# Where two FFN passes meet: another bank is copied first, and the weight splits queue elsewhere

## The chip, the cores and the metric

The kernel runs on one core of one Trainium2 chip, as one program. The metric is the device time in microseconds (us) of one execution, and the time of a version is the median of its runs. Every duration below comes from one profiled execution of the kernel before.

## What is computed

The reference is a two-layer causal decoder trunk on an input of 512 tokens by 1024 features. Each layer has an attention mixer and then a gated FFN with a short causal convolution, and each part is normalised and added back to the input. The change is in the down projection of the FFN, in both layers:

```python
def conv_ffn(h, w_up, conv_w, conv_b, w_down):
    u = causal_dwconv(h @ w_up, conv_w, conv_b)
    gate, up = jnp.split(u, 2, axis=-1)
    return (jax.nn.silu(gate) * up) @ w_down      # (512, 2816) @ (2816, 1024)
```

## The kernel before, in words

**Exact products from pairs.** Every fp32 operand is split into a high part and a remainder. ACT casts the high part (line 83 for weights, line 225 for activations) and DVE subtracts it (lines 84 and 226). A product is then three matmuls on PE: high by high (line 320), remainder by high (321), high by remainder (322), in `mm3`. Names with h at the end (`wh`, `gh`) are high parts, names with l (`wl`, `gl`) are remainders.

**Down projection with seven products in place of eight.** The 2816 rows are 22 blocks, which are taken as 11 pairs, and the tokens are taken in two halves s = 0 and s = 1. In *phase one* the loop over k (11 steps) accumulates four PSUM banks for each half: d, a, b and c, eight products of three matmuls in a step, 24 matmuls. In the last step (k = 10) the four banks of a half are summed into the tile `uu`: ACT copies one bank (line 689) and DVE adds the other three (line 691). In *phase two* the loop over n (11 steps) goes on accumulating into a, b and c without clearing them, six products in a step in the order a, b, c of half 0 and a, b, c of half 1, 18 matmuls. So the first product of phase two into a bank must wait until that bank has been read for `uu`. I call this place the seam. Bank d is not written in phase two. At the end the outputs are bank a and `uu` less b or c.

**Where the weights come from.** `down_weights` makes one unit of weights at a time. In phase two the unit c of step n is loaded (line 347, queue of SP, into one of three buffers `wraw`), split, and subtracted from a kept tile by DVE (line 340); the result is unit d of step n, which is split too. The activations of phase two are split by `split_later` (lines 225 and 226), whose sources lie in the tiles `hold`. Some of these share their memory with the gain tiles, so the loads of the next gains (line 221) wait until those splits are done. `W.next` hands out a unit, and before that makes units up to `W.depth` ahead. The units that are ahead come earlier in the program's text, and the scheduler, which puts the instructions of each engine in an order, goes by the text, by what is ready in its own reckoning and by free buffers. In phase one the depth is 4; in the last step it is set to 2, so that no further unit is made there, and afterwards it is set back.

Each engine runs its instructions in the order that it was given. In the names of the built program, banks acc_5183 to acc_5186 are d, a, b and c of half 0 in layer 0, and acc_5187 to acc_5190 are the same of half 1. The line numbers below 690 are the same before and after.

Of the kernel before, what the change touches and what calls it, by code (L numbers as in the profile page):

```python
# [13 lines left out]
ALU = mybir.AluOpType  # L14
# [83 lines left out]
def trunk(tc, A, out):  # L98
    nc = tc.nc
    PE, ACT, DVE, POOL = nc.tensor, nc.scalar, nc.vector, nc.gpsimd  # L100

    with ExitStack() as top:
# [15 lines left out]
        def bank(tag, name, *shape):  # L118

            t = pp.tile([P, S], F32, tag=tag, name=name, bufs=BANKS[tag])  # L120
            if not shape:
                return t[:]
            n = math.prod(shape)
            names = "abc"[:len(shape)]
            return t[:, :n].rearrange(f"p ({' '.join(names)}) -> p {' '.join(names)}",
                                      **dict(zip(names, shape)))
# [90 lines left out]
        W = Weights(nc, wpool, units, 5)  # L217

        def gain(name, row):
            g = glob.tile([P, D], F32, tag="gain", name="gain", bufs=2)  # L220
            nc.sync.dma_start(g[:], A[name][row:row + 1, :].partition_broadcast(P))
            return g
# [51 lines left out]
        def part_of(t, ms, n, a, g, between=None, dve_first=False):  # L274

            c = slice(n * S, n * S + S)
            o = t[:, c]
            if isinstance(a, tuple):
                DVE.tensor_tensor(o, *a, ALU.subtract)
                a = o  # L280
            def product():
                DVE.tensor_tensor(o, a, g[:, c], ALU.mult)

            if dve_first:
                product()
            junk = chp.tile([P, D], BF16, tag="junk", name="junk", bufs=1)
            ACT.activation(junk[:, :S], a, AF.Square, scale=D ** -0.5, accum_out=ms[:, n:n + 1])  # L287
            if between:
                between()
            if not dve_first:  # L290
                product()

        def begin(pool=None, tag="s"):
            return ((pool or chp).tile([P, D], F32, tag=tag, name="t", **({"bufs": 2} if tag in ("z", "sp") else {})),
                    begin_sum())
# [91 lines left out]
        def ffn(layer, xnT, pending, final):  # L387
            with ExitStack() as es:
# [141 lines left out]
                def product(o, x, fresh):  # L530
                    nonlocal slot, w
                    if slot % 2 == 0:
                        w = W.next()
                    for k in range(4):
                        b = slice(slot % 2 * S + k * P, slot % 2 * S + (k + 1) * P)
                        xs = [v[:, k] if isinstance(x, list) else v[:, k * 256:(k + 1) * 256] for v in x]
                        mm3(o, w[0][:, b], w[1][:, b], *xs, fresh and k == 0, k == 3, not fresh)
                    slot += 1
# [119 lines left out]
                bk = {(m, s): bank(tags[m][s], "acc") for s in range(2) for m in "dabc"}  # L658
# [8 lines left out]
                def split_later():  # L667
                    k = LATER[len(later)]
                    g = g_tile()
                    if k in whole:  # L670
                        split(g[0][:, :768], g[1][:, :768], home(whole[k])[:, :768])
                    else:
                        vs = [x[:].rearrange("p (a b) -> p a b", b=P) for x in g]
                        for at, src in zip((slice(1, 4, 2), slice(0, 4, 2), slice(4, 6)), hold[k]):
                            split(vs[0][:, at], vs[1][:, at], src)
                    later.append(g)

                for k in range(HF):
                    if k == HF - 1:
                        depth, W.depth = W.depth, 2  # L680
                        uu = sp.tile([P, 2, S], F32, tag="y", name="uu")
                    w1, w2 = W.next(), W.next()
                    for s in range(2):
                        g = early[k]
                        for m, at, w, half in (("d", 7 - s, w2, 0), ("a", 3 - 2 * s, w1, 0),
                                               ("b", 2 - 2 * s, w2, 1), ("c", 5 - s, w1, 1)):
                            product(m, s, g, at, w, half, k == 0, k == HF - 1)
                        if k == HF - 1:
                            ACT.copy(uu[:, s], bk["d", s])
                            for m in "abc":  # L690
                                DVE.tensor_tensor(uu[:, s], uu[:, s], bk[m, s], ALU.add)  # L691
                    if k < 3:

                        ACT.copy(t2[k], w2[0][:, :S].bitcast(F32))
                        DVE.tensor_tensor(t2[k], t2[k], w2[1][:, :S].bitcast(F32), ALU.add)
                    if k >= HF - 3:
                        split_later()
                W.depth = depth
                PLAN = {"a": (lambda s: 3 - 2 * s, 0, 0), "b": (lambda s: 5 - s, 0, 1), "c": (lambda s: 2 - 2 * s, 1, 0)}

                def later_product(m, s, n, ws, part=slice(0, S), fresh=False):
                    at, w, half = PLAN[m]
                    product(m, s, later[n], at(s), ws[w], half, fresh and n == HF - TAIL, n == HF - 1, not fresh, part)

                early_q = []
                for n in range(HF - TAIL):
                    ws = [W.next(), W.next()]
                    if len(later) < HF:
                        split_later()
                    for s in range(2):  # L710
                        for m in "abc":
                            later_product(m, s, n, ws)
                    if n == 2:
                        g_post = gain("ffn_post_g", layer)
                        if not final:
                            g_next = gain("od_pre_g", 0)
                    if n == 4:
                        for z in range(2):
                            early_q.append(begin(sp, "y"))
                            part_of(*early_q[z], 1, uu[:, z], g_post)  # L720
                    if n == 5:
                        for i in ORDER:
                            X[i] = glob.tile([P, D], F32, tag=f"X{i}", name=f"X{i}")
                            nc.sync.dma_start(X[i][:], spill[i * P:(i + 1) * P, :])
# [3 lines left out]
                ws = [[W.next(), W.next()] for _ in range(TAIL)]  # L728
                nx = None if final else new_xnT()

                def bank_done(m, s, *part, between=None):
                    for n in range(TAIL):
                        later_product(m, s, HF - TAIL + n, ws[n], *part)
                        if between and n == 1:
                            between()
                    return bk[m, s]

                if final:
# [15 lines left out]
                    with tc.manual_schedule(engines={DVE.engine, ACT.engine, POOL.engine}):  # L754
# [3 lines left out]
                        a = bank_done("a", 0)  # L758
# [19 lines left out]
                        a = bank_done("a", 1)  # L778
# [1105 lines left out]

        xnT = even()
        xnT = ffn(0, *xnT, False)
        xnT = odd(*xnT)
        ffn(1, *xnT, True)


# [100 lines left out]
```

## Time and profile before

| | |
|---|---|
| median of 3 runs | 1109.82 us (1108.27 to 1109.95) |
| profiled execution | 1108.7 us |
| its span, first to last instruction | 1106.8 us, so 1.9 us lie around it |
| mean granted clock of PE | 0.998 |
| PE, DVE, ACT busy in the span | 99%, 81%, 58% |
| phase one of layer 0 ends, phase two begins | 516.9 us from the span's start |
| the same in layer 1 | 1054.5 us |

A row of the timeline gives start, duration, engine, source line, operation, tiles and shapes, and in brackets how long the engine stood idle before it and what ended that. Equal neighbours are merged with a count. PE is matmuls and PEld the loading of their stationary operand. The duration of a matmul is modelled and matmuls overlap, so the distance from start to start is what one costs. At both seams every matmul has its row, so matmuls can be counted there.

### The profile page before, as it was taken

Reading aid. Unit: us, or ns where it says so; the run is one execution under the profiler, and the core shown is the slowest. Engines: PE = TensorE matmul, PEld = TensorE weight load, DVE = VectorE, ACT = ScalarE, POOL = GpSimd, SP = SyncE. Lnnn points to the kernel's source line nnn. Section 1 sums busy time; section 2 is a strip of 40 time slices with the busy share of each in tenths; the row PEclk is TensorE's granted clock in tenths of the full one; section 3 lists DMA queues with packets and bytes.
Section 4 is the critical chain, followed back from the end, with each engine's and each line's share of the span. In section 5 each row is a group of like instructions: output and inputs, shape, how many; then the busy total and the mean of one; then the engine's idle time right before and its main releaser. Section 6 shows DMA issues by size and latency. Waiting matters only on the chain.

```text
span 1106.8 us, 17950 instructions
## 1 busy us (share of the span) xinstructions
PE 1097.0 (99%) x6688; PEld 953.7 (86%) x6688; DVE 897.5 (81%) x1509; ACT 642.0 (58%) x1094; POOL 129.5 (12%) x246
## 2 busy tenths in 40 slices
PE   9999999999999999999999999999999999999997
PEld 8876777898999999887888877888999999988876
DVE  6676676498999999999874765458989999999896
ACT  6555666346666665556544655555566666656562
POOL 3211043220000000000032111014100000000002
PEclk9999999999999999999999999999999999999999
DMA  7897898457556555354727999858756555534462
GB/s 273 262 240 210 230 291 229 112 182 190 186 177 191 178 183 181 124 181 138 247 84 262 287 295 302 212 175 243 197 157 191 182 179 184 188 122 157 152 209 77
DMA packets 72600, 217.51 MB, mean 197 GB/s; under 512 B 10048, under 2 KB 11200, under 8 KB 64320
## 3 DMA queue, kind: packets, MB, share of 16 engines
q1 hardware_dynamic: 61872, 147.99, 40.3%
q0 software_dynamic: 9920, 67.12, 24.2%
q10 hardware_dynamic: 720, 1.25, 0.3%
q8 instruction: 53, 0.87, 0.3%
q14 instruction: 35, 0.29, 0.1%
HBM read 208.95 MB, written 73.43 MB: 255 GB/s over the span
## 4 chain that ended last, share of the span: by engine, by line
PE 86%; DVE 8%; DMA 3%; ACT 2%; issue 1%; POOL 0%; POOLq 0%; DVEq 0%; SPq 0%; ACTq 0%
PE u L322 12%; PE u L320 12%; PE u L321 12%; PE acc L320 3%; PE acc L321 3%; PE acc L322 3%; DVE wl L84 3%; PE apt L320 3%; PE apt L321 3%; PE apt L322 3%; PE ao L320 2%; DMA wraw<-in_ffn_w_down 2%; PE ao L322 2%; PE ao L321 2%; PE aqk L320 1%
## 5 line engine op out<-in xcount | busy, mean ns | idle before, releaser
L84 DVE TENSOR_TENSOR wl<-wraw,wh 128x1024 fp32r<-128x1024 f32 x246 | 298.2, 1219 | 33.5 <-ACT wh L83 32.9
L83 ACT CAST wh<-wraw 128x1024 fp32r<-128x1024 f32 x246 | 254.1, 1046 | 105.4 <-PE u L321 23.9
L322 PE MATMUL u<-xh,wl 128*128 128x256 f32 (+1 forms) x640 | 194.9, 305 | 0.0
L321 PE MATMUL u<-xl,wh 128*128 128x256 f32 (+1 forms) x640 | 194.8, 305 | 0.0
L320 PE MATMUL u<-xh,wh 128*128 128x256 f32 (+1 forms) x640 | 194.5, 305 | 0.0
L322 PEld LDWEIGHTS u<-xh,wl 128*128 128x128 f32 x640 | 122.2, 191 | 5.5 <-DVE wl L84 0.7
L321 PEld LDWEIGHTS u<-xl,wh 128*128 128x128 f32 x640 | 122.2, 191 | 4.9
L320 PEld LDWEIGHTS u<-xh,wh 128*128 128x128 f32 x640 | 122.0, 191 | 5.0
L320 PE MATMUL u<-gh,wh 128*128 128x256 f32 x384 | 108.7, 283 | 0.0
L322 PE MATMUL u<-gh,wl 128*128 128x256 f32 x384 | 108.7, 283 | 0.0
L321 PE MATMUL u<-gl,wh 128*128 128x256 f32 x384 | 108.6, 283 | 0.0
L320 PE MATMUL acc<-wh,gh 128*128 128x512 f32 (+1 forms) x234 | 90.4, 389 | 0.6 <-DVE uu L691 0.6
L321 PE MATMUL acc<-wl,gh 128*128 128x512 f32 (+1 forms) x234 | 90.9, 388 | 0.0
L322 PE MATMUL acc<-wh,gl 128*128 128x512 f32 (+1 forms) x234 | 90.6, 387 | 0.0
L233 POOL TENSOR_TENSOR rv<-ms,epst 128x1 f32<-128x1 f32 x31 | 11.8, 382 | 619.0 <-ACT junk L287 287.6
L484 ACT ACTIVATE y<-u,cw 128x512 f32<-128x512 f32 x88 | 67.7, 777 | 26.5 <-PE u L322 26.4
L321 PEld LDWEIGHTS u<-gl,wh 128*128 128x128 f32 x384 | 73.7, 192 | 0.1
L320 PEld LDWEIGHTS u<-gh,wh 128*128 128x128 f32 x384 | 73.7, 192 | 0.1
L322 PEld LDWEIGHTS u<-gh,wl 128*128 128x128 f32 x384 | 73.7, 192 | 0.0
L163 POOL DMA_DIRECT2D ws<-in_ffn_up_q x72 | 51.8, 721 | 158.5 <-DMA ws<-ws 74.7
L490 DVE SCALAR_TENSOR_TENSOR y<-u,cw,y 128x510 f32<-128x510 f32 x88 | 65.5, 747 | 2.2
L488 DVE SCALAR_TENSOR_TENSOR y<-u,cw,y 128x511 f32<-128x511 f32 x88 | 65.1, 743 | 1.2 <-ACT y L484 1.2
(382 smaller groups left out, 2456.4 us busy)
## 6 DMA issues: line engine op xcount, KB each, us to landing
ws<-in_ffn_up_q POOLq DMA_DIRECT2D x48, 768.0 KB, 12.7
wraw<-ws SPq DMA_DIRECT2D x128, 256.0 KB, 2.9
wraw<-in_ffn_up_q SPq DMA_DIRECT2D x96, 256.0 KB, 2.9
wraw<-in_ffn_w_down SPq DMA_DIRECT2D x44, 512.0 KB, 3.5
ws<-ws POOLq DMA_DIRECT2D x16, 768.0 KB, 13.3
ws<-in_ffn_up_q POOLq DMA_DIRECT2D x24, 512.0 KB, 6.7
wraw<-in_ffn_w_up SPq DMA_DIRECT2D x24, 512.0 KB, 4.7
wraw<-in_od_w_dqk SPq DMA_DIRECT2D x12, 512.0 KB, 10.0
```

Of the source, the lines that this page charges most:

```text
L83: self.nc.scalar.copy(h[:, :w], raw[:, :w])
L84: self.nc.vector.tensor_tensor(l[:, :w], raw[:, :w], h[:, :w].bitcast(F32), ALU.subtract)
L163: nc.gpsimd.dma_start(tiles[j][c][:].rearrange(wide, q=4), src.rearrange(wide, q=4), accum_op=op, max_dma_last_dim=8192)
L233: POOL.tensor_tensor(v[:, :n], ms, eps[:, :n], ALU.add)
L320: PE.matmul(o, lh, rh, start=first, stop=False, skip_group_check=more)
L321: PE.matmul(o, lh, rl, start=False, stop=False, skip_group_check=more)
L322: PE.matmul(o, ll, rh, start=False, stop=last, skip_group_check=more)
L484: ACT.activation(y[:, z], u[z], AF.Identity, bias=c[:, 3:4], scale=c[:, 2:3])
L488: DVE.scalar_tensor_tensor(y[:, z, 1:], u[z][:, :S - 1], c[:, 1:2], y[:, z, 1:], ALU.mult, ALU.add)
L490: DVE.scalar_tensor_tensor(y[:, z, 2:], u[z][:, :S - 2], c[:, 0:1], y[:, z, 2:], ALU.mult, ALU.add)
```

## The change

Three things change in the text of `ffn`, and with it in both layers.

1. In the last step of phase one ACT copies bank a in place of d, and DVE adds b, c and d in place of a, b and c.
2. The depth is no longer lowered in that step, so the units d of step 0 and c of step 1 are made before the sums.
3. The next units are made inside `tc.issue_after(mark)`: an instruction of the block goes on its engine behind the mark. The marks are the copy of bank a (ACT) and the addition of bank c (DVE), of half 0 for d of step 1 and of half 1 for c of step 2. Nothing else is ordered.

```diff
                 for k in range(HF):
                     if k == HF - 1:
-                        depth, W.depth = W.depth, 2
+                        marks = []
                         uu = sp.tile([P, 2, S], F32, tag="y", name="uu")
...
                         if k == HF - 1:
-                            ACT.copy(uu[:, s], bk["d", s])
-                            for m in "abc":
-                                DVE.tensor_tensor(uu[:, s], uu[:, s], bk[m, s], ALU.add)
+                            taken = [ACT.copy(uu[:, s], bk["a", s])]
+                            for m in "bcd":
+                                taken.append(DVE.tensor_tensor(uu[:, s], uu[:, s], bk[m, s], ALU.add))
+                            marks.append((taken[0].ins, taken[2].ins))
...
-                W.depth = depth
+
+                def behind(s):
+                    es = ExitStack()
+                    for mark in marks[s]:
+                        es.enter_context(tc.issue_after(mark))
+                    return es
+
...
                 early_q = []
+                with behind(0):
+                    W.ahead(W.pos + W.depth)
                 for n in range(HF - TAIL):
-                    ws = [W.next(), W.next()]
+                    with behind(1) if n == 0 else ExitStack():
+                        ws = [W.next(), W.next()]
```

What the scheduler made of it is the same in both layers. On DVE, at the seam of layer 0, the rows from the subtraction for unit d of step 3 (`t2_5275`) to the last addition stood like this:

```order
L340 TENSOR_TENSOR t2_5275<-t2_5275,wraw_5691 128x512
L84 TENSOR_TENSOR wl_5646<-wraw_5647,wh_5645 128x1024
L691 TENSOR_TENSOR uu_5600<-uu_5600,acc_5184 128x512
L84 TENSOR_TENSOR wl_5657<-wraw_5658,wh_5656 128x1024
L691 TENSOR_TENSOR uu_5600<-uu_5600,acc_5185 128x512
L691 TENSOR_TENSOR uu_5600<-uu_5600,acc_5188 128x512
L691 TENSOR_TENSOR uu_5600<-uu_5600,acc_5186 128x512
L691 TENSOR_TENSOR uu_5600<-uu_5600,acc_5189 128x512
L84 TENSOR_TENSOR wl_5690<-wraw_5691,wh_5689 128x1024
L691 TENSOR_TENSOR uu_5600<-uu_5600,acc_5190 128x512
```

Now the same stretch of DVE reads (wl_5606 is what was wl_5646, unit c of step 1; gl_5653 is unit d of step 1, gl_5664 the activations of step 3):

```order
L84 TENSOR_TENSOR wl_5606<-wraw_5607,wh_5605 128x1024
L340 TENSOR_TENSOR t2_5275<-t2_5275,wraw_5691 128x512
L691 TENSOR_TENSOR uu_5600<-uu_5600,acc_5185 128x512
L691 TENSOR_TENSOR uu_5600<-uu_5600,acc_5186 128x512
L84 TENSOR_TENSOR gl_5653<-hold_5173,gh_5652 128x512
L691 TENSOR_TENSOR uu_5600<-uu_5600,acc_5183 128x512
L691 TENSOR_TENSOR uu_5600<-uu_5600,acc_5189 128x512
L226 TENSOR_TENSOR gl_5664<-hold_3531,gh_5663 128x768
L691 TENSOR_TENSOR uu_5600<-uu_5600,acc_5190 128x512
L340 TENSOR_TENSOR hold_5173<-hold_5173,wraw_5658 128x512
L691 TENSOR_TENSOR uu_5600<-uu_5600,acc_5187 128x512
L84 TENSOR_TENSOR wl_5657<-wraw_5658,wh_5656 128x1024
```

The three long splits of weights that stood among the additions (wl_5646, wl_5657, wl_5690) are out of them: the first has moved ahead of the subtraction, the other two (steps 2 and 3) behind the last addition. Banks b and c of half 0 are added first, and bank d comes after the banks that phase two needs.

On ACT the rows around the two copies (line 689) stood like this:

```order
L83 CAST wh_5645<-wraw_5647 128x1024
L689 COPY uu_5600<-acc_5183 128x512
L83 CAST wh_5656<-wraw_5658 128x1024
L83 CAST gh_5718<-t2_5275 128x512
L225 CAST gh_5729<-hold_4047 128x768
L689 COPY uu_5600<-acc_5187 128x512
L83 CAST wh_5689<-wraw_5691 128x1024
```

They now stand like this, with bank a in place of d and fewer casts ahead of the second copy:

```order
L83 CAST wh_5605<-wraw_5607 128x1024
L689 COPY uu_5600<-acc_5184 128x512
L83 CAST gh_5652<-hold_5173 128x512
L225 CAST gh_5663<-hold_3531 128x768
L689 COPY uu_5600<-acc_5188 128x512
L83 CAST wh_5656<-wraw_5658 128x1024
L83 CAST wh_5689<-wraw_5691 128x1024
```

The cast of step 2's weights has gone from between the copies to behind both. On the queue of SP, which issues the loads, the piece ahead of the seam stood like this:

```order
L221 DMA gain_5751<-in_ffn_post_g 128x1024
L347 DMA wraw_5523<-in_ffn_w_down 128x1024
L347 DMA wraw_5525<-in_ffn_w_down 128x512
L221 DMA gain_5753<-in_od_pre_g 128x1024
L347 DMA wraw_5567<-in_ffn_w_down 128x1024
L347 DMA wraw_5647<-in_ffn_w_down 128x1024
L347 DMA wraw_5658<-in_ffn_w_down 128x1024
L347 DMA wraw_5691<-in_ffn_w_down 128x1024
```

It is now:

```order
L347 DMA wraw_5523<-in_ffn_w_down 128x1024
L347 DMA wraw_5525<-in_ffn_w_down 128x512
L347 DMA wraw_5567<-in_ffn_w_down 128x1024
L347 DMA wraw_5607<-in_ffn_w_down 128x1024
L347 DMA wraw_5658<-in_ffn_w_down 128x1024
L221 DMA gain_5751<-in_ffn_post_g 128x1024
L221 DMA gain_5753<-in_od_pre_g 128x1024
L347 DMA wraw_5691<-in_ffn_w_down 128x1024
```

The two gain loads have moved behind five and three loads of weights, to just ahead of wraw_5691 (step 3's weights), because the activations of step 2, whose split frees the gains' memory, are now split there and no longer earlier in phase one. In layer 1 only the first gain is loaded at this place. PE's products keep their order, but for one interchange: the first matmul of step 1 no longer stands ahead of the last product of step 0.

## The prediction

> **What bounds the kernel now.** I read the page first, for the engine that sets the span:
>
> ```profile
> PE 1097.0 (99%) x6688; PEld 953.7 (86%) x6688; DVE 897.5 (81%) x1509; ACT 642.0 (58%) x1094; POOL 129.5 (12%) x246
> PE 86%; DVE 8%; DMA 3%; ACT 2%; issue 1%; POOL 0%; POOLq 0%; DVEq 0%; SPq 0%; ACTq 0%
> ```
>
> PE is busy 99% of the span and holds 86% of the chain that ended last. A change that adds no matmul and removes none can gain only where PE stands still. So the second question is where PE waits around the change. The view of waits, for PE and for its loads of stationary operands, answers for layer 0 (480 to 575 us) and then for layer 1 (1015 to 1090 us):
>
> ```profile
> PE acc L320 <- DVE uu L691: 0.8, 2, 0.6
> PEld acc L320 <- DVE uu L691: 1.9, 3, 1.0
> ...
> PEld acc L320 <- DVE uu L691: 1.2, 3, 0.7
> PE acc L320 <- DVE uu L691: 0.2, 1, 0.2
> ```
>
> These are the only waits of PE in the two stretches, and all of them end with an addition into `uu`. The seam is the one place to gain, and nothing else near it is late today.
>
> How much is lost is read from the starts of matmuls in the timeline, first in layer 0:
>
> ```profile
> 512.16 0.39 PE L320 MATMUL acc<-wh,gh 128*128 128x512 f32 x1
> 516.92 0.39 PE L320 MATMUL acc<-wh,gh 128*128 128x512 f32 x1
> 518.36 0.50 PE L320 MATMUL acc<-wh,gh 128*128 128x512 f32 x1 [0.60 <-DVE uu L691]
> 519.55 0.50 PE L320 MATMUL acc<-gh 128*128 128x512 f32 x1 [0.22 <-DVE uu L691]
> 523.83 0.40 PE L320 MATMUL acc<-gh 128*128 128x512 f32 x1
> ```
>
> The first two rows are the same bank a of half 0: its last product in phase one, and its first in phase two. Between them are 21 matmuls in 4.76 us, so one costs 0.2267 us and a product of three 0.68 us. Bank a runs on time. Bank b (518.36) should start at 517.60, and bank c (519.55) waits again. The last row is 24 matmuls after 516.92. Without a wait they take 5.44 us, here 6.91: **1.47 us are lost in layer 0**. The bracketed 0.60 and 0.22 are less, since a matmul's modelled duration hides the rest. The same in layer 1:
>
> ```profile
> 1054.49 0.39 PE L320 MATMUL acc<-wh,gh 128*128 128x512 f32 x1
> 1056.41 0.50 PE L320 MATMUL acc<-gh 128*128 128x512 f32 x1 [0.23 <-DVE uu L691]
> 1060.69 0.40 PE L320 MATMUL acc<-gh 128*128 128x512 f32 x1
> ```
>
> From 1054.49 to 1060.69 there are again 24 matmuls, 6.20 us less 5.44: **0.76 us are lost in layer 1**.
>
> Why the additions are late is read from DVE's rows at the seam of layer 0:
>
> ```profile
> 511.68 0.95 DVE L226 TENSOR_TENSOR gl<-hold,gh 128x768 fp32r<-128x768 f32 x1
> ...
> 514.14 0.69 DVE L340 TENSOR_TENSOR t<-t,wraw 128x512 f32<-128x512 f32 x1
> 514.75 1.22 DVE L84 TENSOR_TENSOR wl<-wraw,wh 128x1024 fp32r<-128x1024 f32 x1
> 515.89 0.68 DVE L691 TENSOR_TENSOR uu<-uu,acc 128x512 f32<-128x512 f32 x1
> 516.48 1.22 DVE L84 TENSOR_TENSOR wl<-wraw,wh 128x1024 fp32r<-128x1024 f32 x1
> 517.62 2.47 DVE L691 TENSOR_TENSOR uu<-uu,acc 128x512 f32<-128x512 f32 x4
> 520.01 1.22 DVE L84 TENSOR_TENSOR wl<-wraw,wh 128x1024 fp32r<-128x1024 f32 x1
> 521.15 0.68 DVE L691 TENSOR_TENSOR uu<-uu,acc 128x512 f32<-128x512 f32 x1
> ```
>
> DVE runs without a gap here. From start to start an addition costs 0.60 us, a long split 1.14 (514.75 to 515.89), the split of 768 columns 0.87 (it is 0.08 shorter than its duration, as the others are). The banks had been complete long before; what makes the additions late is the three long splits between them, and the order (bank a of half 1 ahead of c of half 0).
>
> **The change part by part.** *The copy of another bank* costs nothing by itself. The view of the tile `uu` in layer 0 shows what is there; the numbers of copies and additions do not change:
>
> ```profile
> L691 DVE TENSOR_TENSOR uu<-uu,acc x6: 679/680/681, 515.9 to 521.1; 128x512 f32<-128x512 f32 x6
> L689 ACT COPY uu<-acc x2: 580/582/584, 514.0 to 516.7; 128x512 f32<-128x512 f32 x2
> ```
>
> Bank a of half 0 is complete at 513.0 (its third matmul starts two steps of 0.2267 after 512.16 and takes 0.39), so ACT, whose queue then holds only short casts, can copy it by 513.7. Bank a of half 1 is complete 12 matmuls later, at 515.7, and copied by about 516.4. Phase two wants these banks at 516.92 and 518.96. This takes two additions out of the way of PE.
>
> The row of a cast of weights on ACT, which the next step needs:
>
> ```profile
> 513.06 1.05 ACT L83 CAST wh<-wraw 128x1024 fp32r<-128x1024 f32 x1
> ```
>
> *The new order of DVE*, with the same durations. It begins with the subtraction for step 3, which waits for its load. That load is issued when the split of wl_5566 frees its buffer, which is as early as before, so I let the row start at 514.14 again. The split of wl_5606 has to be done by then. It follows its cast on ACT, which must wait until PE has left a buffer of step 9: its last reader there, b of half 1, stands seven matmuls ahead of 512.16 and ends at 511.0. A cast takes 1.05, a split 1.22, so this is done at about 513.4. From 514.14 on:
>
> - b of half 0: starts 514.74, ends 515.4; wanted at 517.60
> - c of half 0: ends 516.0; wanted at 518.28
> - the split gl_5653 (0.60) and bank d (0.60) pass
> - b of half 1: starts 517.14, ends 517.8; wanted at 519.64
> - the split gl_5664 (0.87) passes
> - c of half 1: starts 518.6, ends 519.3; wanted at 520.32
>
> Every bank is free ahead of PE, the closest by 1.0 us, so all of the 1.47 us goes. In layer 1 the same subtraction stands earlier against PE:
>
> ```profile
> 1051.01 0.68 DVE L340 TENSOR_TENSOR t<-t,wraw 128x512 f32<-128x512 f32 x1
> ```
>
> It starts 3.48 us before phase two there, against 2.78 in layer 0, so the margins are 0.7 larger, and the 0.76 us goes too.
>
> *The later splits* become later. Step 2's weights (wl_5657) were done at 517.70 and are now the work after the last additions: a subtraction (0.60, from 519.2), the addition of d, then the split from 520.4 to 521.6. PE wants it 36 matmuls after 516.92, at 525.08, 3.4 us later. Unit d of step 2 follows at 522.3, wanted at 526.4; step 3 at about 523.4, wanted at 529.2. The buffer that this frees takes step 5's load 3.9 us later than before; by the group of these loads (3.5 us, below), it lands at 525.2, and PE wants it at 537.3. These margins hide the delay; if they were used up, each us would cost one.
>
> *The gain loads* now run just ahead of step 3's load. What such loads take is not shown in this neighbourhood, so I bound it by groups of the view of transfers:
>
> ```profile
> wraw<-in_ffn_w_down SPq DMA_DIRECT2D x44, 512.0 KB, 3.5
> X<-spill SPq DMA_DIRECT2D x8, 512.0 KB, 7.0
> gain<-in_ffn_post_g SPq DMA_DIRECT2D x2, 512.0 KB, 4.5
> ```
>
> A load of weights takes 3.5 us in the median, and the X tiles, issued four at a time, 7.0. Step 3's load can be later by 0 to 3.5 us. I take 0 to 1, as by the gains' 4.5, since the gains start 3 us ahead of it. That stays within the margin of 1.0.
>
> The sum is −1.47 −0.76 = −2.23 us. The profiled execution of 1108.7 us would be 1106.5; it lies 1.1 us under the median of the runs, 1109.82, from which I count: **1107.6 us**. Bounds: PE cannot give back more than it loses, so −2.2 is the best at this place, and 0 is the worst that the additions alone could bring.
>
> **The rivals.** *One addition stays late.* Everything in the new order hangs on a load that stands in front of all additions. If it lands 1.5 us late, c of half 1 ends at 520.8 in layer 0, and PE loses 0.5 there, and 0.1 for a restart (0.50 against 0.39 in the rows of 518.36 and 512.16); layer 1 stays free. That gives 1108.2. For it speaks the smallest margin; against it that two of the six banks have moved to ACT.
>
> *The gain is given back later.* Layer 0's 1.47 us comes half a span before the end. If something between is paced by transfers and not by PE, it is lost again, and 0.76 remains: 1109.1. Against it: POOL, which issues the long transfers, has 0% of the chain.
>
> *Slower: the load collides with the gains.* If step 3's load takes the 7.0 us of the X tiles, the additions are 3.5 us late. In layer 0 b of half 0 would be 1.3 late, c of half 1 2.5 in all, with two restarts 2.7; in layer 1, 1.8 and 0.2, so 2.0. That is 4.7 against 2.23 now: 1112.3. It decides from about 3.4 us of delay on; below 2.3 us there is still a gain. Against it: in layer 1 only one gain is loaded there, and X loads come in fours, gains in twos. For it: the Trainium skill, "DMA: Bandwidth & Descriptors", section "Issuing engines are not separate DMA queues", says that transfers run on the same 16 DMA engines and interleave, whoever started them. By that rule the gains do slow the load, for as long as they are in flight together. The 7.0 against 3.5 agrees, but no row here has two gains ahead of a load at this distance.
>
> *The change does not do what it says.* The order of the program excludes this: bank a is read by ACT and no long split is left between the additions.
>
> **How the numbers follow.** Forecast, all stalls gone, 1107.6: 0.64. One addition late, 1108.2: 0.14. Given back, 1109.1: 0.13. Slower, 1112.3: 0.09. About 0.2%, 2.2 us, is what a measurement can tell from no change, and the forecast of 2.23 stands on that line. Its weight I divide 0.36 to 0.28 in favour of faster, since layer 0 loses twice what layer 1 does, so the wait varies, and the median run is longer than the profiled one. That gives faster 0.36, within 0.2% 0.55, slower 0.09. The range reaches from 1106.0 (the lowest run, 1108.27, less 2.23) to 1110.4, which takes in all but the collision and a half us above no gain at all, as the runs spread.
>
> **What would show it.** Right: no wait of PE for L691 in either layer; 24 matmuls from phase two's first in 5.4 to 5.5 us; both copies done before phase two; the split of wl_5657 past 520 us. Wrong: a wait of PE that ends with c of half 1 (late load), with a split of line 84 (later weights), or a load of line 347 near 511 us that takes over 5 us. A total that moves by much less than the two seams do would show the gain given back.

## The result and the profile after

After the change the median is 1112.13 us (1110.13 to 1113.83, 14 runs), before it 1109.59 (1108.27 to 1111.59, 14 runs). The ratio is 1.0023 (95% interval 1.0016 to 1.003): **slower by about 2.5 us**, where 2.2 us faster was forecast. The profiled execution after took 1111.91 us, with a span of 1110.0.

I follow the order of the prediction. The page first: the busy time of PE and DVE.

```profile
PE 1098.2 (99%) x6688; PEld 955.0 (86%) x6688; DVE 897.7 (81%) x1509; ACT 641.6 (58%) x1094; POOL 128.0 (12%) x246
PE 85%; DVE 8%; DMA 3%; ACT 2%; issue 1%; POOL 0%; POOLq 0%; DVEq 0%; ACTq 0%; SPq 0%
```

DVE does as much as before (897.5 us), and nothing on the page stands out. The view of waits does, for PE and its loads from 440 to 580 us and then, for PE, from 990 to 1110 (engine, what waits, who ended it: us in total, times, longest):

```profile
PE acc L321 <- DVE wl L84: 1.4, 1, 1.4
PE tp L268 <- DVE t L821: 1.0, 1, 1.0
...
PEld acc L320 <- DVE uu L691: 0.4, 1, 0.4
...
PE acc L321 <- DVE wl L84: 0.8, 1, 0.8
```

The waits for an addition (line 691) are nearly gone. New ones have come: for a split of weights (line 84) in both layers, and for the next layer's normalised rows (line 821). The seam itself, in the timeline of PE after, first and 25th matmul of phase two and the one late between them, then the two of layer 1:

```profile
517.62 0.39 PE L320 MATMUL acc<-wh,gh 128*128 128x512 f32 x1
...
521.17 0.50 PE L320 MATMUL acc<-gh 128*128 128x512 f32 x1
...
523.35 0.39 PE L320 MATMUL acc<-gh 128*128 128x512 f32 x1
...
1057.32 0.39 PE L320 MATMUL acc<-wh,gh 128*128 128x512 f32 x1
...
1062.76 0.39 PE L320 MATMUL acc<-gh 128*128 128x512 f32 x1
```

24 matmuls take 5.73 us in layer 0 (6.91 before) and 5.44 in layer 1 (6.20). **The seams gained 1.18 and 0.76 us**, 1.94 of the 2.23 forecast. So the loss is elsewhere. DVE's rows at the seam of layer 0, after:

```profile
509.12 1.22 DVE L84 TENSOR_TENSOR wl<-wraw,wh 128x1024 fp32r<-128x1024 f32 x1
510.25 0.42 DVE L226 TENSOR_TENSOR gl<-hold,gh 128x256 fp32r<-128x256 f32 x1
512.79 1.23 DVE L84 TENSOR_TENSOR wl<-wraw,wh 128x1024 fp32r<-128x1024 f32 x1 [2.12 <-ACT wh L83]
515.77 0.69 DVE L340 TENSOR_TENSOR t<-t,wraw 128x512 f32<-128x512 f32 x1 [1.76 <-DMA wraw<-in_ffn_w_down]
516.38 1.48 DVE L691 TENSOR_TENSOR uu<-uu,acc 128x512 f32<-128x512 f32 x2
...
520.44 0.68 DVE L691 TENSOR_TENSOR uu<-uu,acc 128x512 f32<-128x512 f32 x1
```

DVE stands idle twice, **2.12 us for ACT's cast and 1.76 us for step 3's load**, 3.88 us in all, where it had no gap before. The first is inherited from ACT, whose cast waits at the head of its queue until PE has left a buffer. The other casts of this place are queued behind it, as their splits are on DVE:

```profile
511.70 1.05 ACT L83 CAST wh<-wraw 128x1024 fp32r<-128x1024 f32 x1 [3.38 <-PE acc L322]
```

The view of stretches shows the same as busy time (length; busy of PE, PEld, DVE, ACT, POOL with counts; clock; DMA share; GB/s). Before:

```profile
500.00:510.00 10.00, 10.00 (x46) 8.29 (x45) 7.97 (x10) 7.36 (x9) 0.00 (x0) 1.00 0.44 154
510.00:516.00 6.00, 6.00 (x28) 4.96 (x27) 6.00 (x9) 4.20 (x7) 0.00 (x0) 1.00 0.29 87
1050.00:1056.00 6.00, 6.00 (x27) 4.57 (x25) 6.00 (x9) 5.17 (x8) 0.00 (x0) 1.00 0.35 108
```

After:

```profile
500.00:510.00 10.00, 10.00 (x46) 8.29 (x45) 8.85 (x12) 6.92 (x10) 0.00 (x0) 1.00 0.56 157
510.00:516.00 6.00, 6.00 (x28) 4.98 (x27) 2.12 (x4) 2.90 (x4) 0.00 (x0) 1.00 0.80 274
1050.00:1056.00 6.00, 6.00 (x29) 4.95 (x28) 3.20 (x5) 2.90 (x4) 0.00 (x0) 1.00 0.56 174
```

From 500 to 516 us DVE does 10.97 us of work in place of 13.97: 3.0 us fall behind. Where that comes due is 35 us later, at the weights of step 10, the last one. In the timeline before, of DVE (the first of the two long splits is this one; two small ones follow it) and PE:

```profile
544.01 2.35 DVE L84 TENSOR_TENSOR wl<-wraw,wh 128x1024 fp32r<-128x1024 f32 x2
546.28 1.28 DVE L84 TENSOR_TENSOR gl<-t,gh 128x512 fp32r<-128x512 f32 x2
...
549.23 0.39 PE L321 MATMUL acc<-wl,gh 128*128 128x512 f32 x1
```

And after, with the two small splits ahead, and with what follows at the transition to layer 1 (one row is ACT's):

```profile
546.13 0.69 DVE L84 TENSOR_TENSOR gl<-t,gh 128x512 fp32r<-128x512 f32 x1
...
547.87 0.69 DVE L84 TENSOR_TENSOR gl<-t,gh 128x512 fp32r<-128x512 f32 x1
...
549.07 1.22 DVE L84 TENSOR_TENSOR wl<-wraw,wh 128x1024 fp32r<-128x1024 f32 x1
550.35 0.50 PE L321 MATMUL acc<-wl,gh 128*128 128x512 f32 x1 [1.38 <-DVE wl L84]
...
554.09 1.05 ACT L83 CAST wh<-wraw 128x1024 fp32r<-128x1024 f32 x1 [1.15 <-DMA wraw<-in_od_w_v]
555.17 1.23 DVE L84 TENSOR_TENSOR wl<-wraw,wh 128x1024 fp32r<-128x1024 f32 x1 [0.95 <-ACT wh L83]
...
564.39 1.32 PE L268 MATMUL tp<-ident,t 128*128 128x128 f32 x8 [1.05 <-DVE t L821]
```

The sum closes. Before, the split ended at 545.23 and was wanted at 549.23: a lead of 4.00 us. The run after is 0.70 us late as a whole at the seam (517.62 against 516.92; about 0.5 of it arises in the first 35 us of the span and 0.2 near 237 us, far ahead of the change), so the split is 550.29 − 545.93 = 4.36 us later, and PE, which lost 1.18 less at the seam, wants it 1.18 sooner: 4.00 − 1.18 − 4.36 = −1.54. PE's start moves by about that (the bracket shows 1.38, the rest lies in the modelled duration). Of the 4.36 us, 3.0 are the time that fell behind. Another 1.2 are the two small splits of 0.60 that the scheduler now puts ahead of this one (operands of c in steps 8 and 9, wanted later). The long split at 555.17 belongs to the next layer's weights; it waits for a cast on ACT, which waited for its load, and it holds up DVE's rows of the normalisation, for which the transposes wait. That last link is read from this one profile; no experiment below isolates it.

### The profile page after: what moved, and what is told of

It reads as the page before. It is cut to its first block, busy times and chain, and to the rows that moved or that the text cites. A ratio compares the mean times of both kernels' runs of the same rounds, so it can differ in the third digit from the quotient of the medians.

```text
span 1110.0 us, 17954 instructions
## 1 busy us (share of the span) xinstructions
PE 1098.2 (99%) x6688; PEld 955.0 (86%) x6688; DVE 897.7 (81%) x1509; ACT 641.6 (58%) x1094; POOL 128.0 (12%) x246
## 4 chain that ended last, share of the span: by engine, by line
PE 85%; DVE 8%; DMA 3%; ACT 2%; issue 1%; POOL 0%; POOLq 0%; DVEq 0%; ACTq 0%; SPq 0%
PE u L322 12%; PE u L321 12%; PE u L320 12%; PE acc L321 3%; PE acc L320 3%; PE acc L322 3%; PE apt L320 3%; PE apt L321 3%; PE apt L322 3%; DVE wl L84 2%; DMA wraw<-in_ffn_w_down 2%; PE ao L320 2%; PE ao L322 2%; PE ao L321 2%; PE aqk L320 1%; PE p L322 1%
```

## The experiments

All compare with the kernel before on the same chip. "VectorE" in the expectations is DVE. The theories: **D**, DVE's idle time ahead of the additions is the loss, since DVE has few us of slack from there to the end of phase two. **R**, the late splits of c in steps 2 and 3 hold the three buffers of the loads. **G**, the gain loads beside step 3's load. **C**, the copy of bank a is not free. **O**, the order at the end of phase two. An edit moves the numbers of the lines behind it by a few: line 691 is also 692, 694 or 700 below, and in one run lines 268, 320 and 321 are one higher. In the expectations of three runs the split of step 10 is called that of the last step but two; the times show that it is this one.

The table has the ratio, DVE's busy us of the six at each seam, and the us that PE loses: the start of the same matmul, after less ahead of the place, against "the copy alone", in whose profile PE itself waits nowhere from 440 us on (its loads 0.2 us at a time, about 0.14 us in all at the seam of layer 0, so that a minus is possible).

| kernel | ratio (95%) | DVE 510–516 | DVE 1050–1056 | lost at the seams | at step 10 and the transition | at step 10, layer 1 |
|---|---|---|---|---|---|---|
| before | 1 | 6.00 | 6.00 | 1.36 + 0.78 | 0 | 0 |
| after | 1.0023 (1.0016–1.003) | 2.12 | 3.20 | 0.15 | 1.76 + 1.55 | 1.15 |
| copy alone | 0.9981 (0.9973–0.999) | 5.93 | 6.00 | 0 | 0 | 0 |
| after, no marks | 0.9993 (0.9984–1.0002) | 5.83 | 5.83 | 0.11 + 0.75 | 0 | 0 |
| order alone | 1.0011 (1.0002–1.002) | 2.72 | 3.96 | 0.58 | 0.92 + 1.46 | 0.92 |
| after, gains late | 0.9995 (0.9986–1.0004) | 3.78 | 5.21 | −0.13 | 0.91 + 1.08 | 1.21 |
| copy, late splits | 0.999 (0.9981–0.9998) | 6.00 | 6.00 | 1.01 + 0.42 | 0 | 0 |
| before, more DVE | 1.0028 (1.0017–1.0039) | 6.00 | 6.00 | 1.07 + 0.91 | 1.48 + 0.03 | 0.26 |

After against before is 4.61 − 2.14 = 2.47 us by this table, and 2.54 by the medians.

**The copy alone** (the kernel before, with the sums of the change):

```diff
-ACT.copy(uu[:, s], bk["d", s])
-for m in "abc":
+ACT.copy(uu[:, s], bk["a", s])
+for m in "bcd":
```

> The copy alone: ACT copies bank a instead of bank d, the three additions are b, c, d; the later weights' splits stay ordered as in the kernel before. Theory D (VectorE's time): what cost time after the change is that VectorE stood idle ahead of the additions (2.12 us busy of the 6 from 510 to 516 us, 6.00 before), and VectorE has little slack from there to the end of phase two. Here VectorE keeps its old queue, so no idle time ahead of the additions and no wait of PE for a split of weights; bank c of half 0 is free at about the time PE wants it, so the seam loses 0 to 0.2 us in layer 0, nothing in layer 1: 1109.6 - 2.0 = 1107.6. Theory G (the gain loads beside step 3's load): the same, the gains stay early. Theory C (the copy of bank a itself is late or holds ACT's casts): no gain at the seam or waits for line 689, 1109.6 or more.

1107.14 us, ratio 0.9981: 2.1 us faster, as D and G say. C falls. The window of the seam, and all that is left of waits there:

```profile
510.00:516.00 6.00, 6.00 (x28) 4.95 (x28) 5.93 (x8) 3.88 (x7) 0.00 (x0) 1.00 0.31 94
```

```profile
PEld acc L320 <- DVE uu L691: 0.2, 1, 0.2
```

DVE keeps its work ahead of the additions, and PE itself does not wait.

**After, without the marks**:

```diff
 def behind(s):
     es = ExitStack()
-    for mark in marks[s]:
-        es.enter_context(tc.issue_after(mark))
     return es
```

> The kernel after without the marks: the later splits are not tied behind the addition of bank c, everything else of the change stays (the copy of bank a, no lowered depth of the look-ahead, the gain loads ahead of step 3's load). VectorE then does five pieces of later work ahead of the additions. Theory D (VectorE's idle time, made by the marks): VectorE is busy for 5.5 us or more of 510 to 516, no wait for splits at the end of phase two; the splits among the additions may cost 0 to 1 us at the seam: 1107.0 to 1108.5. If the idle time comes from the depth and not from the marks: as after the change, 1111 to 1112.

1108.23 us. DVE's idle time is gone, with the gain loads still where the change puts them:

```profile
510.00:516.00 6.00, 6.00 (x28) 4.99 (x27) 5.83 (x9) 3.74 (x5) 0.00 (x0) 1.00 0.73 231
```

Nothing waits at the end of either phase two. So the marks made the idle time: by the two ratios they cost 0.0030, 3.3 us. What is still lost, against the copy alone, lies at the seams.

**The order alone** (after, but ACT copies bank d and DVE adds a, b, c).

> The order alone: the later weights' splits stand behind the additions as after the change, but ACT copies bank d and VectorE adds a, b, c. Theory D: VectorE idles ahead of the additions as after the change (3 to 4 us between 510 and 516), so the weights come late at the end of both phases two as after (4 to 4.5 us lost), and the seam gains less than with the copy, 0 to 1.5 of 2.2: 1112.5 to 1114. Theory C: 1108 to 1109.6, as the copy was the fault. Theory G: about as after, 1112.

1110.82 us, below D's range (from 1112.5 on): the places behind the seams lost 3.30 us where I had 4 to 4.5, and the seams gained 1.56 us against before where I had at most 1.5. PE's waits in layer 0 are those of the change, and one for an addition:

```profile
PE tp L268 <- DVE t L821: 0.9, 1, 0.9
PE acc L321 <- DVE wl L84: 0.6, 1, 0.6
PE acc L320 <- DVE uu L691: 0.2, 1, 0.2
```

**After, with the gain loads late:**

```diff
+with tc.issue_after(W.down_loads[-1].ins):   # load of step 4
     g_post = gain("ffn_post_g", layer)
```

> The kernel after, with the two gain loads put behind step 4's load of weights, so that nothing of theirs is in flight with step 3's load. Step 3's load should land 3.2 to 3.7 us after its issue instead of 5.06. Theory G (the gains cost it): all of the loss goes, 1107.6 to 1108. Theory D: only the part of VectorE's idle time goes that the load ended, 1.8 of 3.9 us; the other 2.1, for the cast of wl_5606, stays, so the waits for splits shrink but do not vanish: about 1110.0. Theory R (the late splits of step 2's and 3's weights hold the three buffers of the loads, and so every later load is late): no change beside the 0.3 us at the seam, 1111.8.

1108.51 us, between G and D. DVE's rows show that one of the two waits has gone, as D says:

```profile
512.51 1.23 DVE L84 TENSOR_TENSOR wl<-wraw,wh 128x1024 fp32r<-128x1024 f32 x1 [2.11 <-ACT wh L83]
513.66 0.68 DVE L341 TENSOR_TENSOR t<-t,wraw 128x512 f32<-128x512 f32 x1
```

The load took 3.06 us from the end of its issue to landing, not 5.06. But 3.1 us of the loss go by the ratios, not 2.1. The profiled run (1110.0) is one of the longest; its waits at the end are smaller than after in layer 0 (1.99 against 3.31 us), not in layer 1 (1.21 against 1.15). A reading that is not shown, since the shorter runs left no profile: with the lead nearly used up, a run falls on one side or the other.

**The copy alone, with the gain loads near** (the reverse: behind the load of c in step 2).

> The copy alone, with the two gain loads put just ahead of step 3's load, as the change puts them, and nothing else moved. Step 3's load should take about 5 us in layer 0 instead of 3.28, so VectorE's subtraction that waits for it, and all additions behind, start 1.6 to 1.8 us later. With the copy alone bank c of half 0 was free just in time, so PE loses 1.4 to 1.8 us at the seam of layer 0; in layer 1, with one gain, 0 to 0.7. VectorE idles 1.7 us, which its lead of 4.4 us covers, so nothing is lost behind the seam. Theory D: 1107.1 + 1.4 to 2.4 = 1108.5 to 1109.5. Theory G in its strong form (the gains make the loss at the end of phase two): waits for splits of weights as after the change, 1111.

1106.92 us, ratio 0.9971 (0.9961 to 0.9981): a miss. The load took 4.04 us, not 5, and landed at 514.89; the edit had also moved the subtraction that needs it behind a long split and the first addition, to 516.95, so DVE never waited for it. G in its strong form falls: gains at that place cost nothing where DVE has something else to do.

**Before, with more DVE work**, six repeats of one split behind the additions:

```diff
 split(g[0][:, :768], g[1][:, :768], home(whole[k])[:, :768])
+if len(later) == 4:
+    for _ in range(6):
+        DVE.tensor_tensor(g[1][:, :768], home(whole[k])[:, :768],
+                          g[0][:, :768].bitcast(F32), ALU.subtract)
```

> The kernel before, with one split of 768 columns (later row block 4) done six times more, between the last addition and step 5's weights in each layer: 6 x 0.87 = 5.2 us of VectorE's time and nothing else, neither a load nor an order is changed ahead of it. Theory D: VectorE has 3 to 4 us of slack from the seam to the end of phase two, so this is late at the same rows as after the change: PE waits for the last weights' split (1 to 1.6 us in layer 0, 0.5 to 1 in layer 1) and for the transposes and first weights of layer 1 (1 to 1.5): 1109.6 + 3 to 4 = 1112.6 to 1113.6. Theories G and R: VectorE's time alone costs nothing, 1109.6 to 1110.

1111.82 us, 2.4 us slower by the medians and 3.1 by the ratio, where D had 3 to 4. Nothing is changed ahead of the seam, and the same wait appears at step 10:

```profile
PE acc L321 <- DVE wl L84: 1.1, 1, 1.1
PE acc L320 <- DVE uu L694: 0.5, 2, 0.3
```

Its split ended at 550.43, 5.20 us later than before. (The two small splits stood ahead of it here too, 1.2 us, and a gap of 1.59 us that DVE had ahead of 537.59 had shrunk to 0.41.) So work added to DVE is enough for this wait, with the order that the scheduler then makes. The transposes did not wait here (0.03), so that part of the loss is not reproduced.

**The copy alone, with the splits of steps 2 and 3 behind the additions:**

```diff
-W.split(h, l, c, 1024)
+with tc.issue_after(W.mark) if n in (4, 6) else ExitStack():   # W.mark: the last addition of bank c
+    W.split(h, l, c, 1024)
```

> The copy alone, and the splits of step 2's and step 3's weights alone put behind the last addition of bank c, so that VectorE has other work to do ahead of the additions and does not stand idle. Theory D (VectorE's idle time): VectorE is busy for nearly all of 510 to 516 us, its total work is the same, so the split of the last step but two, which PE wants first at about 548.5, ends at 544 to 545 as with the copy alone, and the time is that of the copy alone within 0.4 us: 1106.8 to 1107.5. Theory R (late splits hold the three buffers of the loads): the loads from step 5's on are issued 3 to 4 us later, that split ends at 547 to 548.5, with waits of 0 to 1 us for it and up to 1.5 behind it: 1107.5 to 1109.5.

1108.33 us, above D's range, but not for R's reason. Step 5's load was issued at 523.22, nearly as late as after the change (523.49; 517.73 before), and yet nothing waits for a split at step 10. All that PE loses lies at the seam, since the scheduler put other splits between the additions:

```profile
PE acc L320 <- DVE uu L692: 0.6, 2, 0.3
```

The split of step 10 ended at 546.86, against PE 1.6 us later than in the copy alone, and the lead of 4.4 us there covers that. R falls as the cause of the waits.

**How much slack there is** was asked with three and six repeats on the copy alone.

> The copy alone, with the split of row block 4 (768 columns) done three times more in each layer, behind the additions: 3 x 0.87 = 2.6 us of VectorE's time. With the copy alone the split of the last step but two ended 4.4 us (layer 0) and 4.25 us (layer 1) ahead of its use. Theory D: its lead falls to about 1.8 and 1.6 us, nothing waits for it, and the time stays within 0.5 us of the copy alone: 1107.1 to 1107.6. If VectorE's time were a cost from the first microsecond on: 1109 or more.

> The same with six repeats, 5.2 us: more than the lead of 4.4. Theory D: the split of the last step but two is 0.8 to 1.5 us late in layer 0 and 0.3 to 1.2 in layer 1, and layer 1's first transposes or weights 0 to 1.5 late: 1107.1 + 1.5 to 3.5 = 1108.6 to 1110.6. Theories G and R (VectorE's time alone costs nothing): 1107.1 to 1107.6.

1110.0 us (ratio 1.0005, 0.9996 to 1.0014) and 1115.23 (1.0043, 1.0027 to 1.0059). Both miss upward: 2.6 us of work cost 2.7 us by the ratios, where D had expected next to nothing. With three repeats the row that shows why is DVE's, and ACT's ahead of it:

```profile
540.79 0.69 DVE L84 TENSOR_TENSOR gl<-t,gh 128x512 fp32r<-128x512 f32 x1 [1.74 <-ACT gh L83]
```

```profile
539.18 1.05 ACT L83 CAST wh<-wraw 128x1024 fp32r<-128x1024 f32 x1 [4.30 <-DMA wraw<-in_ffn_w_down]
```

Step 9's load took 5.14 us there (3.24 in the copy alone); the cast that waits for it stands ahead of the cast that DVE needs, and DVE idles another 1.74. The two small splits had moved ahead of step 10's too. 2.6 + 1.74 + 1.2 is 5.5, more than the lead of 4.4. So the lead is not a reserve of 4.4 us of work, as D had it: a delay also changes the scheduler's order and what the loads meet. Why the load took 3.24 us in some kernels and 5.1 in others was not settled.

**The subtractions on POOL** (after, line 340 moved to the idle engine):

```diff
-sub(d, d, c[:, lo])
+POOL.tensor_tensor(d, d, c[:, lo], ALU.subtract)
```

> The kernel after, with the subtractions of line 340 (11 in each layer, 128x512) done by POOL, which is idle from 500 to 550 us, instead of VectorE: 11 x 0.60 = 6.6 us of VectorE's time saved in each layer, and the additions no longer stand behind the wait for step 3's load. The splits stay behind the additions. Theory D: more than the 3.9 us of idle time is given back, so no or little waiting for splits at the end of phase two: 1107 to 1108.5, if POOL takes no more than about 2 us for one (no row shows it; the margin of the splits behind them is what decides). Theory R (the late splits hold the loads): as after, 1111 to 1112.

1113.31 us (ratio 1.0041, 1.0027 to 1.0055), slower still. A row of POOL, and DVE's splits of 768 columns alone and beside POOL:

```profile
525.17 1.77 POOL L377 TENSOR_TENSOR t<-t,wraw 128x512 f32<-128x512 f32 x1 [4.80 <-DMA wraw<-in_ffn_w_down]
```

```profile
523.10 0.95 DVE L226 TENSOR_TENSOR gl<-hold,gh 128x768 fp32r<-128x768 f32 x1
...
525.71 2.04 DVE L226 TENSOR_TENSOR gl<-hold,gh 128x768 fp32r<-128x768 f32 x1
```

The split lasts 1.09 us longer, about what POOL still has to run when it starts (1.23). Between 500 and 560 us the long splits' mean goes from 1.22 to 1.52 us, and DVE is not relieved at all (busy 54.1 of these 60 us, 51.4 after the change): the test of D that I meant did not take place. The Trainium skill, "SBUF — State Buffer", section "SBUF: two separate sides", says that POOL and a DVE operation with two SBUF inputs lock out each other for a whole instruction; these rows agree, and so does the addition with one input in PSUM, at 0.68 us as ever. Step 10's split stood in its old place here and was waited for all the same, which speaks against O.

**The order at the end**, once put back in the kernel after (small splits behind step 10's), once put into the copy alone:

```diff
-W.split(h, l, held.pop(k), S)               # after: steps 8 and 9, now done behind step 10's split
+W.put_off.append(((h, l), held.pop(k)))
...
-W.split(h, l, c, 1024)                      # copy alone: step 10's split behind the small ones
+with tc.issue_after(W.small) if n == 2 * HF - 2 else ExitStack():
+    W.split(h, l, c, 1024)
```

> The kernel after, with two small splits (512 columns, the second stationary operands of steps 8 and 9) put behind the split of the last step's weights on VectorE, as they stood before the change; the change had moved them ahead of it. Theory D (VectorE's idle time ahead of the additions, 3.9 us in layer 0 and 2.8 in layer 1, is the loss): the last step's split comes only 2 x 0.60 = 1.2 us sooner, so of 1.76 us of waiting in layer 0 about 0.5 stays, of 1.15 in layer 1 nothing, and the 1.55 us at the transposes of the next layer stays, since the two splits still stand ahead of it: 1112.1 - 2.4 = 1109.7, 1109.2 to 1110.5. Theory O (the order at the end of phase two is the loss: every kernel so far with the small splits ahead waits there, every one with the old order does not): all waits at the end go, 1107.3 to 1108.0.

> The copy alone, with the split of the last step's weights put behind the same two small splits, so that VectorE's order at the end of phase two is the unfavourable one, while VectorE does not idle ahead of the additions. The two small splits wait for casts that stand late on ACT, so the last step's split ends at about 547.8 instead of 544.1, wanted at 548.5. Theory D: nothing waits, 1107.0 to 1107.6. Theory O: PE waits 1 to 1.8 us in layer 0 and about 1 in layer 1, 1109 to 1110.

1110.53 us (1.0014, 1.0005 to 1.0022) and 1108.29 (0.9989, 0.9981 to 0.9998). With the old order the waits of PE in layer 0 are still there, in a profiled run (1112.62) that is one of the longest:

```profile
PE tp L269 <- DVE t L830: 1.8, 1, 1.8
PE acc L322 <- DVE wl L84: 0.9, 2, 0.8
PE acc L321 <- DVE uu L700: 0.5, 1, 0.5
```

In layer 1 they are gone, as D says. In layer 0 PE loses 1.53 us at step 10 where D had 0.5, and 2.3 at the transition where D had 1.55; so the median, far above O's range, lies at the upper end of D's. The reverse has no such wait in its profiled run (1107.02 us), though its runs spread up to 1110.38. By the ratios the order is worth 0.9 to 1.0 us on either base, but the intervals with and without it overlap. O can be a part, as D's sum has it (1.2 of 4.36), and is not the cause.

## Why the prediction was wrong

**The step that failed is "the later splits": "These margins hide the delay."** I followed the delay to step 5 (wanted 12.1 us after its load) and stopped. DVE is busy for almost all of the next 30 us, so nothing made up for it, and the smallest margin of a split in layer 0 was step 10's, 4.00 us before.

**Its root is in the step before, the new order of DVE.** I wrote that in the kernel before "DVE runs without a gap here", and then let the new queue wait until 514.14 for a load, and earlier for a cast on ACT, at no price, because every bank was still free in time. Both waits came nearly as I had put them. With the 0.70 us of the run taken off, the cast ended at 512.05, where I had 512.1, and the load landed at 515.05 in place of 514.14. So about 2.9 of the 3.88 us of idle time lie in my own times, and 0.9 in the later load. The 3.0 us of work that used to stand there were moved behind the additions, and I put their delay at nothing.

- *The copy of another bank costs nothing*: right. The copy alone brings 2.1 us (1.1 to 3.0 by the interval), and the forecast sum was 2.23.
- *Every bank is free ahead of PE, the closest by 1.0 us*: right in layer 1. In layer 0 the last addition that PE needs (c of half 1) ended at 521.12, against PE 1.1 us later than I had it, most of it from the later load, and 0.29 us stayed.
- *The gain loads, 0 to 1 us*: right by luck. Step 3's load took 5.06 us against 3.20, 1.9 more, but it was issued 0.9 sooner against PE, so it landed only 0.9 later.
- *The rivals*: 1112.3 for the collision is near the result, but by another mechanism. It put the loss at the seam, where 1.94 us were gained. "Given back later" had the right place in time and the wrong cause (transfers), and no loss beyond the gain. "One addition stays late" is what layer 0 showed, at 0.29 us in place of 0.6.
- Two signs named as wrong are what the profile shows: a wait "with a split of line 84 (later weights)", and a load of line 347 near 511 us that takes over 5 us.

The best version of the study is the copy alone, without the marks and with the depth as before: 1107.14 and 1106.92 us in its two forms.

## What to carry to other kernels

An engine that is busy 81% of the span can be all but full for 35 us on end; there, a wait at the head of its queue costs what the work behind it is worth at the next deadline, even if what it waits for is still in time. So when an edit orders work behind a mark, list what the engine did in that place before and follow it to the last consumer, not to the next one. A gain on the critical engine also brings its later deadlines nearer by as much.

## What the hardware showed beside that

With six repeats PE waited 2.04 us for step 9's split and 1.32 us for step 10's, and for a while it ran at half speed: the granted clock was 0.50 from 550.8 to 557.6 us, and matmuls stood 0.427 us apart in place of 0.227.

```profile
550.01 0.50 PE L321 MATMUL acc<-wl,gh 128*128 128x512 f32 x1 [2.04 <-DVE wl L84]
...
552.36 0.80 PE L321 MATMUL acc<-wl,gh 128*128 128x512 f32 x1 [1.32 <-DVE wl L84]
...
553.37 0.63 PE L320 MATMUL acc<-gh 128*128 128x512 f32 x1
553.80 0.63 PE L321 MATMUL acc<-gl,gh 128*128 128x512 f32 x1
```

That added about 2.5 us to the 6.5 that its waits cost in the two layers. The clock had fallen before the second wait began (551.04), 0.8 us after the first had ended, so the two need not add up for it. Single waits of 1.38 us after the change and of 1.84 in the run with the old order at the end did not do this. The Trainium skill, "TensorE: Matmul & The Clock Gate", section "Part 1: The HAM clock gate (the "warmup" mystery)", gives a clock that is halved after an idle window of about 3.4 us. The 0.427 us agree with half the clock, and the 6.8 us that it lasted are twice 3.4; but PE stood idle for only 2.04 us between its matmuls at 547.58 and 550.01, so a whole idle window did not precede it here.
